# One operation over two PSUM banks in the feed-forward, and the first four tiles of a mixer side by side

## The chip, the core and the metric

The kernel runs on one core of a Trainium2 chip. The metric is the device time of one execution in microseconds, as a median of several. TensorE (PE in the profile) multiplies into PSUM, eight banks of 128 partitions by 512 fp32 columns. VectorE (DVE) and ScalarE (ACT) read PSUM; GpSimd (POOL) works on SBUF alone; SyncE (SP) issues most transfers.

## The reference

A trunk of two layers over T = 528 tokens (16 learned ones and 512 given) of 1024 features:

```
h = layer_norm(ALPHA * h + 0.5 * swiglu(h, ffn1_w_up, ffn1_w_down))
h = layer_norm(ALPHA * h + hybrid_mixer(h, ...))
h = layer_norm(ALPHA * h + 0.5 * swiglu(h, ffn2_w_up, ffn2_w_down))

swiglu(x, w_up, w_down):  gate, up = split(x @ w_up);  (silu(gate) * up) @ w_down
hybrid_mixer:  gated sum of a short convolution and latent attention, both from x @ w_in
```

The feed-forward is 2816 features wide. All is fp32. The 16 learned tokens are dropped from the output.

## The kernel before

Features lie on the partitions: x is held as eight tiles of 128 features by 528 tokens, split into a high part `xh` and a low part `xl` (both fp32r), and `r` is the fp32 residual. Every product is made by `mm3` (lines 91 to 93): three matmuls, high by high, high by low and low by high, into the same PSUM bank. Tokens go in two parts, 256 and 272 wide (or two of 256 in the last mixer and the last feed-forward).

Weights come by SP into `raw` tiles of 128x1024 and `operand` splits them: ACT casts to `wh` (line 111), DVE subtracts to `wl` (line 114). There are four `raw` and four `wh`/`wl` buffers.

A feed-forward (`ffn`) begins with `up_start`, which makes four feature tiles plainly while the norm before it still ends its second token part (`pending`, a generator whose steps are called between the products), and makes the differences of x that the rest needs (`combos`, on POOL, line 338). Then `up_seven` is called nine times, 36 times in the whole kernel. It makes two feature tiles of gate and up for two token halves out of seven half-deep products in place of eight. In order: g1 by x1a into `pa`, g1' by t2 into `pb`, the down projection of earlier features (`mid[0]`, into the other PSUM name `pf`), g2 by x2a on top of `pa`, u1 by t3 on top of `pb`, u2 by nt4 on top of `pb`, s1 by t1 into `pc`, more down projection, g2' by x2b on top of `pc`. Each of these is two groups (j = 0, 1), one to a bank. Between the products DVE and ACT read the sums: after t3 the two adds of line 447 make `u3s` from `pb`, and only then may nt4 add to the same banks:

```
product(pb, operand(u1), t3, False)
for j in range(2):
    V.tensor_tensor(u3s[j], pb[j], m1[j], op=ALU.add)
product(pb, operand(u2), nt4, False)
```

The last down projection adds to `r` (line 572), feeds the sums of the norm (`Norm.add`: squares on ACT at line 262, sums on DVE and POOL at lines 270 and 271), and for its second token part calls a step of the norm of the first part after each tile.

`Norm.run` makes, per token part, the sums over features by matmuls (`token_sums`, line 206), the mean and a reciprocal root by a chain of small DVE operations (lines 282 to 285 and 222 to 231), and lays them out along the tokens by `spread`: ACT scales an identity by one column (line 215) and PE multiplies it by ones (line 216). POOL subtracts the mean (line 293), DVE, ACT and DVE scale and split (lines 301 to 307).

A mixer (`attention`) starts with `first(0)`: four products of x's first token part (`ukv`, `ukr`, two of `ucq`), one after the other, each over all eight tiles of x, with the steps of the norm of the second token part between and after them. Then come two convolution products, the small norms of the latents (`second`, `third`) and `first(1)`.

PSUM is one pool per stage with two names: `ps` (four banks in a feed-forward, six in a mixer) and `pf` (the rest). The tile framework orders each engine's queue by planning the program ahead: among the operations that are ready in its plan it takes the one that comes first in the program. The code holds an operation back where that is not wanted (`tc.issue_after`: behind a given instruction on the same engine). On the chip each queue then runs in that fixed order and waits on semaphores.

Of the kernel before, what the change touches and what calls it, by code (L numbers as in the profile page):

```python
# [18 lines left out]
P = 128  # L19
D = 1024  # L20
# [24 lines left out]
FFN_SCR, MIX_SCR = (4, 14), (6, 8)  # L45
# [6 lines left out]
def trunk(ctx: ExitStack, tc: tile.TileContext, x, meta, f1_up, f1_dn, w_in, b_gate, conv_w, qn_g, w_uq,  # L52
# [12 lines left out]
    @contextmanager  # L65
    def scratch(n, t):

        with tc.tile_pool(name="psp", bufs=1, space=bass.MemoryType.PSUM, reuse_waits="tile") as pool, \
                tc.tile_pool(name="tmp", bufs=t, reuse_waits="tile") as tp:
            banks.append((pool, n))  # L70
            tps.append(tp)
            yield
            banks.pop()
            tps.pop()

    def psum():
        pool, n = banks[-1]
        return pool.tile([P, 512], F32, name="ps", bufs=n)

    def psum2():  # L80
        pool, n = banks[-1]
        return pool.tile([P, 512], F32, name="pf", bufs=8 - n)
# [136 lines left out]
    def rsqrt(v, n, nt, by=float(D)):  # L219
# [10 lines left out]
        V.tensor_scalar(u, u, by / 0.375, 1.875 * by, op0=ALU.mult, op1=ALU.add)  # L230
        return y, V.tensor_tensor(y, u, y, op=ALU.mult)  # L231

    class Norm:
# [10 lines left out]
        def shift_of(self, q0, w):  # L244
# [5 lines left out]
            def shift(i):  # L250
                ps = psum()[:, :w]
# [21 lines left out]
        def run(self, q0, w):  # L273
# [7 lines left out]
            mu, mud, v = small(n, nt), small(n, nt), small(n, nt)  # L281
            V.tensor_copy(mu, mean)
            V.tensor_scalar(mud, mean, float(D), None, op0=ALU.mult)
# [4 lines left out]
            mean, ps = tmp(w), spread(mud, n, nt, psum2())  # L288
# [30 lines left out]

    def project_steps(ps, u, nk, rhs, q0, w, n=4):  # L320
# [8 lines left out]
    def combos(hv, th, tl):  # L329
# [4 lines left out]
        for k in range(KH):  # L334
            a1, b1, a2, b2 = [r[:, m, q:q + w] for m in (k, KH + k) for q in (qa, qb)]
            t1, t2, t3, nt4 = [tmp(w) for _ in range(4)]
            for i, (t, x1, x2) in enumerate(((t1, b1, a1), (t2, b2, t1), (t3, b2, b1), (nt4, a2, t2))):
                G.tensor_tensor(t, x1, x2, op=ALU.subtract)
                split(th[i][:, k, :w], tl[i][:, k, :w], t)

    def up_start(hp, dp, w_up, hv, pending, th, tl, after, begin):
# [12 lines left out]
        def product(o, j, q0, w):  # L354
            ps = psum()[:, :w]
            for k in range(KD):
                mm3(ps, [t[:, k % KH, j * P:(j + 1) * P] for t in o[k // KH]], [t[:, k, q0:q0 + w] for t in (xh, xl)],
                    k == 0, k == KD - 1)
            return ps

        hs = [[hp.tile([P, T], F32R, name=n) for n in ("hh", "hl")] for _ in range(4)]

        def silu(o, j, m, q0, w):
            ps = product(o, j, q0, w)
            sg[m, q0] = tmp(w)
            S.activation(sg[m, q0], ps, AF.Silu)

        def times(o, j, m, q0, w):
            ps = product(o, j, q0, w)
            hh, hl = [t[:, q0:q0 + w] for t in hs[m]]  # L370
# [10 lines left out]
        for part, (q0, w) in enumerate(hv):  # L381
            for f, o in ((silu, g0), (times, u0)):
                for j in range(2):
                    f(o, j, j, q0, w)
                    step(part)
            for j in range(2):
                silu(g1, j, 2 + j, q0, w)
                if after:
                    step(part)
                    step(part)  # L390
# [5 lines left out]
        for q0, w in hv:  # L396
            for j in range(2):
                times(u1, j, 2 + j, q0, w)
                for _ in range(2):
                    next(begin, None)  # L400
        for _ in begin:
            pass
        return hs

    def up_seven(hp, fp, w_up, f, hv, mid, th, tl):
# [9 lines left out]
        def product(ps, u, xs, first):  # L415
            for j in range(2):
                for k in range(KH):
                    mm3(ps[j], [t[:, k, j * P:(j + 1) * P] for t in u], [t[:, k, :] for t in xs],
                        first and k == 0, k == KH - 1, not first)

        def pair():
            return [psum()[:, :w] for _ in range(2)]

        hs = [[hp.tile([P, T], F32R, name=n) for n in ("hh", "hl")] for _ in range(2)]
        m1, u2s, u3s, sg = [[tmp(w) for _ in range(2)] for _ in range(4)]

        pa, pb = pair(), pair()
        product(pa, operand(g1), x1a, True)
        for j in range(2):
            S.copy(m1[j], pa[j])  # L430
# [5 lines left out]
        for j in range(2):  # L436
            V.tensor_tensor(u2s[j], pb[j], m1[j], op=ALU.add)
# [5 lines left out]
        for j in range(2):  # L443
            S.activation(sg[j], pa[j], AF.Silu)
        product(pb, operand(u1), t3, False)
        for j in range(2):
            V.tensor_tensor(u3s[j], pb[j], m1[j], op=ALU.add)  # L447
        product(pb, operand(u2), nt4, False)
        for j in range(2):
            hh, hl = hs[j]  # L450
            V.tensor_tensor(m1[j], pb[j], m1[j], op=ALU.add)
            V.tensor_tensor(sg[j], sg[j], m1[j], op=ALU.mult)
            split(hh[:, qa:qa + w], hl[:, qa:qa + w], sg[j])
        if mid[2]:
            mid[2](hs)
        pc = pair()
# [3 lines left out]
        for j in range(2):  # L460
            V.tensor_tensor(u3s[j], pc[j], u3s[j], op=ALU.add)
# [5 lines left out]
        for j in range(2):  # L467
            hh, hl = hs[j]
            V.tensor_tensor(u2s[j], pc[j], u2s[j], op=ALU.add)
            S.activation(u2s[j], u2s[j], AF.Silu)  # L470
            V.tensor_tensor(u2s[j], u2s[j], u3s[j], op=ALU.mult)
            split(hh[:, qb:qb + w], hl[:, qb:qb + w], u2s[j])
# [736 lines left out]
```

## Time and profile before

| | |
|---|---|
| median of 3 runs | 2213.01 us (2210.86 to 2214.43) |
| the profiled execution | 2215.05 us, of it the span of the profile 2213.0 us |
| mean granted TensorE clock | 0.998 |
| busy in the span | PE 99%, DVE 75%, ACT 44%, POOL 17% |
| DMA | 202.80 MB, mean 92 GB/s |

PE is busy 9 tenths or more in every slice of the page but the first and the last. A matmul's record ends when its pipeline has drained, so records overlap: the rate of matmuls is read from the distance of their starts. "Idle before" counts from the end of the record before.

### The profile page before, as it was taken

How to read it: one execution, taken by the hardware profiler on the slowest of the kernel's cores; microseconds unless marked ns; L12 is line 12 of the kernel's file. 1: busy time of each engine (PE TensorE's matmuls, PEld its weight loads, DVE VectorE, ACT ScalarE, POOL GpSimd, SP SyncE). 2: the span in 40 equal slices, each digit the busy share in tenths (PEclk: the TensorE clock that was granted, in tenths of full speed). 3: DMA queues.
4: the chain of work that ended last, by engine and by line, in shares of the span. 5: the costliest groups of instructions: out<-in, count | busy, mean ns of one | idle time of the engine just before them, and what ended most of it. 6: DMA issues, size and time to landing. Idle time of an engine off the chain costs nothing. (4 is left out here: it accounts for less than half of the span.)

```text
span 2213.0 us, 43882 instructions
## 1 busy us (share of the span) xinstructions
PE 2185.1 (99%) x17989; PEld 2166.9 (98%) x17989; DVE 1663.6 (75%) x3117; ACT 984.7 (44%) x1923; POOL 369.6 (17%) x487
## 2 busy tenths in 40 slices
PE   8999999999999999999999999999999999999998
PEld 8999999999999999999999999999999999999998
DVE  6887788776646788778778877887665568877887
ACT  4343344565533543434453433445655335533341
POOL 3210003301014522000242100033110155100000
PEclk9999999999999999999999999999999999999999
DMA  5333232222233223323323322322222332323322
GB/s 174 96 106 91 91 115 85 77 56 68 68 95 105 68 87 106 105 77 115 105 67 96 105 92 91 115 83 79 56 68 77 94 98 87 95 87 115 96 87 86
DMA packets 240489, 202.80 MB, mean 92 GB/s; under 512 B 6990, under 2 KB 237456, under 8 KB 240288
## 3 DMA queue, kind: packets, MB, share of 16 engines
q1 hardware_dynamic: 237952, 195.65, 29.6%
q0 software_dynamic: 2336, 4.34, 0.8%
q8 instruction: 141, 2.31, 0.4%
q14 instruction: 60, 0.49, 0.1%
HBM read 195.74 MB, written 2.10 MB: 89 GB/s over the span
## 5 line engine op out<-in xcount | busy, mean ns | idle before, releaser
L114 DVE TENSOR_TENSOR wl<-raw,wh 128x1024 fp32r<-128x1024 f32 (+1 forms) x490 | 563.7, 1152 | 235.9 <-ACT wh L111 233.8
L111 ACT CAST wh<-raw 128x1024 fp32r<-128x1024 f32 (+1 forms) x454 | 465.9, 1034 | 575.2 <-PE ps L92 169.4
L91 PE MATMUL ps<-xh,wh 128*128 128x256 f32 (+2 forms) x1760 | 502.2, 285 | 5.2 <-DVE r L572 5.0
L92 PE MATMUL ps<-xl,wh 128*128 128x256 f32 (+2 forms) x1760 | 500.4, 284 | 3.4 <-DVE xl L88 2.8
L93 PE MATMUL ps<-xh,wl 128*128 128x256 f32 (+2 forms) x1760 | 500.3, 284 | 0.0
L91 PEld LDWEIGHTS ps<-xh,wh 128*128 128x128 f32 x1760 | 332.8, 189 | 6.2 <-issue 3.6
L92 PEld LDWEIGHTS ps<-xl,wh 128*128 128x128 f32 x1760 | 332.2, 189 | 5.1 <-DVE xl L88 4.1
L93 PEld LDWEIGHTS ps<-xh,wl 128*128 128x128 f32 x1760 | 332.7, 189 | 0.0
L91 PE MATMUL ps<-th,wh 128*128 128x264 f32 (+1 forms) x1152 | 327.0, 284 | 1.2 <-DVE t L447 1.2
L92 PE MATMUL ps<-tl,wh 128*128 128x264 f32 (+1 forms) x1152 | 325.9, 283 | 0.0
L93 PE MATMUL ps<-th,wl 128*128 128x264 f32 (+1 forms) x1152 | 325.4, 282 | 0.0
L91 PE MATMUL pf<-hh,wh 128*128 128x256 f32 (+1 forms) x864 | 247.3, 286 | 0.0
L93 PE MATMUL pf<-hh,wl 128*128 128x256 f32 (+1 forms) x864 | 246.3, 285 | 0.0
L92 PE MATMUL pf<-hl,wh 128*128 128x256 f32 (+1 forms) x864 | 245.3, 284 | 0.0
L91 PEld LDWEIGHTS ps<-th,wh 128*128 128x128 f32 x1152 | 216.7, 188 | 1.8 <-DVE t L447 1.6
L92 PEld LDWEIGHTS ps<-tl,wh 128*128 128x128 f32 x1152 | 216.9, 188 | 0.0
L93 PEld LDWEIGHTS ps<-th,wl 128*128 128x128 f32 x1152 | 216.5, 188 | 0.0
L91 PE MATMUL pf<-xh,wh 128*128 128x256 f32 (+1 forms) x640 | 187.0, 292 | 0.0
L92 PE MATMUL pf<-xl,wh 128*128 128x256 f32 (+1 forms) x640 | 183.0, 286 | 0.0
L93 PE MATMUL pf<-xh,wl 128*128 128x256 f32 (+1 forms) x640 | 182.3, 285 | 0.0
L91 PEld LDWEIGHTS pf<-hh,wh 128*128 128x128 f32 x864 | 162.8, 188 | 0.0
L93 PEld LDWEIGHTS pf<-hh,wl 128*128 128x128 f32 x864 | 162.8, 188 | 0.0
(323 smaller groups left out, 4836.1 us busy)
## 6 DMA issues: line engine op xcount, KB each, us to landing
raw<-in_ffn_w_up_dram SPq DMA_DIRECT2D x176, 512.0 KB, 3.7
raw<-in_ffn_w_down_dram SPq DMA_DIRECT2D x80, 512.0 KB, 3.4
raw<-in_mix_w_in_dram SPq DMA_DIRECT2D x64, 512.0 KB, 3.8
raw<-in_w_o_dram SPq DMA_DIRECT2D x16, 512.0 KB, 4.0
raw<-in_ffn_w_down_dram SPq DMA_DIRECT2D x16, 256.0 KB, 2.6
raw<-in_w_br_conv_dram SPq DMA_DIRECT2D x8, 512.0 KB, 3.4
raw<-in_w_br_mla_dram SPq DMA_DIRECT2D x8, 512.0 KB, 3.4
out_dram<-r SPq DMA_DIRECT2D x8, 256.0 KB, 2.5
```

The source lines that it names most:

```text
L91: PE.matmul(ps, lhsT=lhs[0], rhs=rhs[0], start=first, stop=False, skip_group_check=more)
L92: PE.matmul(ps, lhsT=lhs[0], rhs=rhs[1], start=False, stop=False, skip_group_check=more)
L93: return PE.matmul(ps, lhsT=lhs[1], rhs=rhs[0], start=False, stop=last, skip_group_check=more)
L111: S.copy(u[0], raw)
L114: V.tensor_tensor(u[1][:, k:k + n], raw[:, k:k + n], u[0][:, k:k + n].bitcast(F32), op=ALU.subtract)
```

## The change

1. In the feed-forward, `ps` is two tiles of two banks (`psum_pair`) in place of four of one. In `up_start`, `up_seven`, `combos` and the last down projection of features, an operation on ACT, DVE or POOL that was done once for each of two feature tiles is done once for both. The temporaries for it are five pairs and four singles in place of 14 singles.
2. The two PSUM names are pools of their own, `pf` in the lower banks in a feed-forward and `ps` in the lower banks in a mixer. The shift of the sums (`shift_of`) and every other sum of the last tokens' down projection use `pf`.
3. `first(0)` of a mixer makes its four products side by side, feature tile by feature tile (`project_all`), and calls the norm's steps after all of them.
4. `spread` multiplies the column itself, repeated along the free side as the stationary operand, by the identity: ACT has no part in it. The mean is laid out by one matmul of ones with the feature sums, and the scaling by D is gone.
5. In the last call of `up_seven` two of the four down projections, not one, leave their second token part for after it.

```
-            dg = tmp(n)[0:n]
-            S.activation(dg, idf[0:n, 0:n], AF.Copy, scale=c[:, i:i + 1])
-            PE.matmul(ps[:, i * n:(i + 1) * n], lhsT=ones[0:n, :], rhs=dg, start=True, stop=True)
+            PE.matmul(ps[:, i * n:(i + 1) * n], lhsT=c[:, i:i + 1].to_broadcast([n, P]), rhs=idf[0:n, 0:n],
+                      start=True, stop=True)
...
-            mean, ps = tmp(w), spread(mud, n, nt, psum2())
+            mean, ps = tmp(w), psum2()[:, :w]
+            PE.matmul(ps, lhsT=ones, rhs=s, start=True, stop=True)
...
+    def project_all(us, nk, rhs, q0, w):
+
+        pss = [psum()[:, :w] for _ in us]
+        for k in range(nk):
+            for ps, u in zip(pss, us):
+                mm3(ps, (u[0][:, k, :], u[1][:, k, :]), (rhs[0][:, k, q0:q0 + w], rhs[1][:, k, q0:q0 + w]),
+                    k == 0, k == nk - 1)
+        return pss
...
-        for k in range(KH):
-            a1, b1, a2, b2 = [r[:, m, q:q + w] for m in (k, KH + k) for q in (qa, qb)]
-            t1, t2, t3, nt4 = [tmp(w) for _ in range(4)]
+        for k in range(0, KH, 2):
+            a1, b1, a2, b2 = [r[:, m:m + 2, q:q + w] for m in (k, KH + k) for q in (qa, qb)]
+            t1, t2, t3, nt4 = [tmp_pair(w) for _ in range(4)]
...
         product(pb, operand(u1), t3, False)
-        for j in range(2):
-            V.tensor_tensor(u3s[j], pb[j], m1[j], op=ALU.add)
+        V.tensor_tensor(u3s, pb, m1, op=ALU.add)
         product(pb, operand(u2), nt4, False)
...
-                    mid = [steps(ci - 1, prev, mp, (0,) if p == 10 and mp == (3,) else (0, 1)) for mp in mps]
+                    mid = [steps(ci - 1, prev, mp, (0,) if p == 10 else (0, 1)) for mp in mps]
...
+                elif j == 1:
+                    rm = r[:, m - 1:m + 1, q0:q0 + w]
+                    V.tensor_tensor(rm, rm, pair, op=ALU.add)
+                    for m1 in (m - 1, m):
+                        norm.add(m1, q0, w)
+                        if part:
+                            step()
...
+                if part == 0:
+                    pss = project_all([ukv, ukr, *ucq], KD, (xh, xl), q0, w)
```

## Rows read from the trace of the kernel before

**Rows 1.** The page's part 1: busy us, share of the span, instructions.

```profile
PE 2185.1 (99%) x17989; PEld 2166.9 (98%) x17989; DVE 1663.6 (75%) x3117; ACT 984.7 (44%) x1923; POOL 369.6 (17%) x487
```

**Rows 2.** Waits of PE: who waited for whom, us in total, times, longest us.

```profile
PE ps L91 <- DVE r L572: 5.0, 3, 1.8
...
PE ps L92 <- DVE xl L88: 2.8, 6, 0.8
...
PE pf L216 <- ACT t L215: 1.3, 2, 0.6
PE ps L91 <- DVE t L447: 1.2, 2, 0.7
...
PE ps L92 <- DVE xl L307: 0.5, 2, 0.3
```

**Rows 3.** Windows, one call of `up_seven`: busy us by engine, clock, DMA.

```profile
139.58:171.71 32.13, 32.13 (x266) 32.13 (x265) 25.54 (x42) 12.46 (x19) 0.00 (x0) 1.00 0.32 99
```

**Rows 4.** Timeline of PE, t3 to nt4: start us, us, what, idle before.

```profile
177.41 0.28 PE L93 MATMUL ps<-th,wl 128*128 128x264 f32 x1
177.52 0.28 PE L91 MATMUL ps<-th,wh 128*128 128x264 f32 x1
```

**Rows 5.** Timeline of DVE, the second add of line 447 there.

```profile
177.72 0.43 DVE L447 TENSOR_TENSOR t<-ps,t 128x264 f32<-128x264 f32 x1 [0.25 <-PE ps L93]
```

**Rows 6.** Groups of DVE by shape: busy us, mean ns, idle before.

```profile
L88 DVE TENSOR_TENSOR hl<-t,hh 128x264 fp32r<-128x264 f32 x108 | 49.1, 454 | 0.6
...
L88 DVE TENSOR_TENSOR tl<-t,th 128x264 fp32r<-128x264 f32 x48 | 26.9, 634 | 0.1
...
L447 DVE TENSOR_TENSOR t<-ps,t 128x264 f32<-128x264 f32 x54 | 23.1, 428 | 5.3 <-PE ps L93 5.1
...
L983 DVE CUSTOM_DVE_ANT_0 ps<-ps,strip 128x512 f32<-128x512 f32 x8 | 5.9, 734 | 0.0
```

**Rows 7.** Timeline of all engines, t3 to nt4 of a first call of `up_seven`.

```profile
79.97 0.28 PE L93 MATMUL ps<-th,wl 128*128 128x264 f32 x1
...
80.28 0.43 DVE L447 TENSOR_TENSOR t<-ps,t 128x264 f32<-128x264 f32 x1
...
80.76 0.39 PE L91 MATMUL ps<-th,wh 128*128 128x264 f32 x1 [0.52 <-DVE t L447]
```

**Rows 8.** Timeline of all engines, a mean laid out in `up_start`.

```profile
754.58 2.04 ACT L215 ACTIVATE t<-idf,sm 68x68 f32<-68x68 f32 x8
...
755.39 0.33 PE L216 MATMUL pf<-t,ones 68*128 68x68 f32 x2
755.53 0.37 PE L93 MATMUL ps<-xh,wl 128*128 128x256 f32 x1
...
756.57 0.36 PE L93 MATMUL ps<-xh,wl 128*128 128x256 f32 x1
```

**Rows 9.** Timeline of PE where the first mixer starts.

```profile
378.39 0.29 PE L93 MATMUL ps<-hh,tl 128*128 128x272 f32 x1
...
380.27 0.35 PE L91 MATMUL ps<-xh,wh 128*128 128x256 f32 x1 [1.59 <-DVE r L572]
...
383.39 0.39 PE L92 MATMUL ps<-xl,wh 128*128 128x256 f32 x1 [0.27 <-DVE xl L307]
```

**Rows 10.** Timeline of DVE at the first mixer's start.

```profile
379.70 0.42 DVE L572 TENSOR_TENSOR r<-r,ps 128x272 f32<-128x272 f32 x1
...
382.86 0.48 DVE L307 SCALAR_TENSOR_TENSOR xl<-r,prm,xh 128x256 fp32r<-128x256 f32 x1
```

**Rows 11.** Timeline of DVE, the chain of the norm's second part in that mixer.

```profile
385.11 0.16 DVE L282 COPY sm<-pf 68x4 f32<-68x4 f32 x1 [1.42 <-PE pf L206]
...
386.27 1.33 DVE L223 TENSOR_SCALAR sm<-sm 68x4 int32<-68x4 int32 x1
...
389.19 0.16 DVE L231 TENSOR_TENSOR sm<-sm 68x4 f32<-68x4 f32 x1
```

**Rows 12.** Windows, after the wait between the two feed-forwards.

```profile
1116.70:1120.10 3.40, 3.40 (x18) 3.40 (x17) 1.27 (x4) 0.43 (x1) 1.56 (x2) 0.50 0.95 297
```

More of the change, by code (lines that the diff above doesn't have):

```diff
@@ L66, in scratch @@
     def scratch(n, t):
-        with tc.tile_pool(name="psp", bufs=1, space=bass.MemoryType.PSUM, reuse_waits="tile") as pool, \
-                tc.tile_pool(name="tmp", bufs=t, reuse_waits="tile") as tp:
-            banks.append((pool, n))
+        with ExitStack() as own:
+            two = {}
+            for name, b in (("ps", n), ("pf", 8 - n))[::1 if n > 4 else -1]:
+                p = own.enter_context(tc.tile_pool(name=name + "p", bufs=1, space=bass.MemoryType.PSUM,
+                                                   reuse_waits="tile"))
+                if name == "ps" and t == FFN_SCR[1]:
+                    two["pp"] = lambda p=p: p.tile([P, 2, 512], F32, name="pp", bufs=2)
+                else:
+                    two[name] = lambda p=p, b=b, name=name: p.tile([P, 512], F32, name=name, bufs=b)
+            tp = own.enter_context(tc.tile_pool(name="tmp", bufs=t, reuse_waits="tile"))
+            banks.append(two)
             tps.append(tp)
@@ L280, in run @@
             ex2 = token_sums(ps, 2 * nt, (q,), n, nt)
[L281 removed]
+            mu, v = small(n, nt), small(n, nt)
             V.tensor_copy(mu, mean)
[L283 removed]
             V.tensor_tensor(v, mu, mu, op=ALU.mult)
@@ L352, in half, with product, silu, times @@
             return us
[L354 to L358, printed above, removed]
-            return ps
[L361 to L365, printed above, removed]
+        def product(o, q0, w, each):
+            ps = psum_pair(w)
+            for j in range(2):
+                for k in range(KD):
+                    mm3(ps[:, j], [t[:, k % KH, j * P:(j + 1) * P] for t in o[k // KH]],
+                        [t[:, k, q0:q0 + w] for t in (xh, xl)], k == 0, k == KD - 1)
+                each()
+            return ps
+        hs = [hidden(hp) for _ in range(2)]
+        def silu(o, m, q0, w, each):
+            ps = product(o, q0, w, each)
+            sg[m, q0] = tmp_pair(w)
             S.activation(sg[m, q0], ps, AF.Silu)
-        def times(o, j, m, q0, w):
-            ps = product(o, j, q0, w)
-            hh, hl = [t[:, q0:q0 + w] for t in hs[m]]
+        def times(o, m, q0, w, each):
+            ps = product(o, q0, w, each)
+            hh, hl = [t[:, :, q0:q0 + w] for t in hs[m]]
             t = sg.pop((m, q0))
@@ L382, in up_start @@
             for f, o in ((silu, g0), (times, u0)):
-                for j in range(2):
[L384 to L390, printed above, removed]
+                f(o, 0, q0, w, lambda: step(part))
+            silu(g1, 1, q0, w, lambda: after and (step(part), step(part)))
             if part == 0:
@@ L396, in up_start @@
         for q0, w in hv:
[L397 to L400, printed above, removed]
+            times(u1, 1, q0, w, lambda: (next(begin, None), next(begin, None)))
         for _ in begin:
             pass
-        return hs
+        return tiles_of(*hs)
     def up_seven(hp, fp, w_up, f, hv, mid, th, tl):
@@ L417, in product @@
                 for k in range(KH):
-                    mm3(ps[j], [t[:, k, j * P:(j + 1) * P] for t in u], [t[:, k, :] for t in xs],
+                    mm3(ps[:, j], [t[:, k, j * P:(j + 1) * P] for t in u], [t[:, k, :] for t in xs],
                         first and k == 0, k == KH - 1, not first)
[L421 to L427, printed above, removed]
+        hh, hl = hidden(hp)
+        hs = tiles_of((hh, hl))
+        m1, u2s, u3s, sg = [tmp_pair(w) for _ in range(4)]
+        pa, pb = psum_pair(w), psum_pair(w)
         product(pa, operand(g1), x1a, True)
-        for j in range(2):
-            S.copy(m1[j], pa[j])
+        S.copy(m1, pa)
         s1 = raw_tile(fp).rearrange("p (k c) -> p k c", c=256)
@@ L435, in up_seven @@
         product(pb, operand(g1), t2, True)
-        for j in range(2):
-            V.tensor_tensor(u2s[j], pb[j], m1[j], op=ALU.add)
+        V.tensor_tensor(u2s, pb, m1, op=ALU.add)
         mid[0]()
@@ L459, in up_seven @@
             mid[3]()
-        for j in range(2):
-            V.tensor_tensor(u3s[j], pc[j], u3s[j], op=ALU.add)
+        V.tensor_tensor(u3s, pc, u3s, op=ALU.add)
         if not mid[2]:
@@ L466, in up_seven @@
             mid[3]()
[L467 to L472, printed above, removed]
+        V.tensor_tensor(u2s, pc, u2s, op=ALU.add)
+        S.activation(u2s, u2s, AF.Silu)
+        V.tensor_tensor(u2s, u2s, u3s, op=ALU.mult)
+        split(hh[:, :, qb:qb + w], hl[:, :, qb:qb + w], u2s)
         return hs
@@ L809, in first, with products @@
                 n, nt = TOKENS[w]
-                ps = psum()[:, :w]
-                project(ps, ukv, KD, (xh, xl), q0, w)
+                if part == 0:
+                    pss = project_all([ukv, ukr, *ucq], KD, (xh, xl), q0, w)
+                else:
+                    pss = (psum()[:, :w] for _ in range(4))
+                def products(u):
+                    ps = next(pss)
+                    if part:
+                        project(ps, u, KD, (xh, xl), q0, w)
+                    return ps
+                pss = iter(pss)
+                ps = products(ukv)
                 S.copy(ckv[:, q0:q0 + w], ps)
```

60 lines of the change are left out of this document (29 added, 31 removed).

## The prediction
> **What bounds the kernel now.** I read the page's busy shares first: PE 99%, DVE 75% [rows 1]. Then one call of `up_seven` by windows: PE is busy 32.13 of 32.13 us and starts a matmul every 32.13/266 = 0.121 us, while DVE has 25.54 us of work and ACT 12.46 [rows 3]. So in these 36 calls, 36 x 32.13 = 1157 us and over half the span, nothing but the number of matmuls sets the time, and work saved on DVE or ACT is worth nothing there. What is left to win lies in PE's waits, and the list of them is short: 5.0 us for line 572, 2.8 and 0.5 us for the low parts of x, 1.3 us for ACT's scaled identities, 1.2 us for line 447 [rows 2]. The reader is to see that these are single places at the seams of the stages, not something that repeats; and that a change here can lose far more by one new wait in each of the 36 calls of `up_seven` than it can win.
>
> **The change part by part**, against the profiled execution's 2215.05 us (a span of 2213.0 and 2.05 around it).
>
> *Merged operations: what they save.* A call of `up_seven` has 18 DVE operations of 128x264, which become 9 of 2x264. One takes 428 ns; the nearest row for the merged one, PSUM in, 512 columns, takes 734 [rows 6], so a pair saves about 0.12 us, a call 9 x 0.12 = 1.1 us and the kernel 36 x 1.1 = 40 us of DVE. Its worth is nought: PE has no gap in that call [rows 3].
>
> *Merged operations: what they cost.* Almost all have cover: `pa` has t2 and the down projection (48 to 72 matmuls, at 0.121 us at least 5.8 us) before it is added to; `pc` has a down projection; a new call's first product (24 matmuls, 2.9 us) covers the read of the pair that its second product takes over. The hidden tiles come later by some 0.3 us for each of five merged operations, 1.5 us, under down projections of 24 matmuls and more; in the last call, where the last down projection needs them at once, the second projection that is now left for later adds 24 matmuls of 2.9 us.
>
> One place has no cover in the program: t3, the add of line 447, nt4 into the same two banks. Before, the first bank is added up while PE fills the second: nt4 starts 0.11 us after t3's last matmul [rows 4], while the second add begins only 0.20 us after nt4's start [rows 5], and nobody waits for it until nt4's second half. Now nt4's first matmul waits for the one add over both banks: it can start no sooner than the second add did, 177.72, takes 0.73 [rows 6], and PE follows 0.05 later (in the first call of all, the add that ended at 80.28 + 0.43 let PE start at 80.76 [rows 7]). 177.72 + 0.73 + 0.05 - 177.52 = 0.98 us, 36 times: 35 us if PE stands still. On DVE the sums of line 451 are queued behind, with slack.
>
> But the planner puts ready work in such holes. Where the mean's four pieces waited for ACT, PE's queue reads two records of line 216, one matmul of the next product, two records, and so on [rows 8]: single matmuls were drawn in. Here the next product in the program, t1 into `pc`, is ready: its weights are split some 10 us ahead, as all are with four buffers, and the banks of `pa` have been read by then. 0.98 us is 8 of its 24 matmuls. What is left is the error of the plan. In rows 8 it erred to the safe side: ACT's eight scaled identities took 2.04 us from 754.58, so the first was there by about 754.9, and PE came to it at 755.39. In rows 7 it erred by 0.67 us (79.97 + 0.12 to 80.76), with DVE behind. Between 0 and 0.98 us a call I take 0.03, near the row with a filled hole: **+1.1 us**, bounds 0 and 35.
>
> The Trainium skill has a rule against this change (Perfetto Trace Analysis, section Optimizing Scalar/DVE Operations): larger operations help where the engine is saturated, and where it is not but makes bubbles on another, operations are to be broken up. DVE at 75% is not saturated [rows 1], so by the rule the merge buys nothing and the 35 us are the price; that is rival 1. The trace agrees with its first half; whether the bubble stays is the planner's doing.
>
> *The start of a mixer.* The last matmul of the feed-forward starts at 378.39, the first of the mixer at 380.27; the next would have been due at 378.52, so 1.75 us are lost, and 0.27 more at 383.39 for the last low part of x [rows 9]. The first wait ends with the read of a PSUM bank at 379.70 + 0.42 [rows 10]; in the new layout the mixer's first four banks are the feed-forward's `pf` banks, idle by then. Side by side, a feature tile of x feeds 12 matmuls, 1.45 us; the last tile, written at 382.86 + 0.48 = 383.34 [rows 10], is needed 84 matmuls after 378.52, at 388.7. Both waits go, and the second mixer has them too (line 572's three waits are 5.0 us, the longest 1.8, and 1.59 is this one: 1.6 is left [rows 2, 9]; line 307's are two of 0.27): 2 x 2.0 = **-4.0 us**, bounds -4.2 and 0.
>
> *What is late next there.* The norm's steps now come behind all 96 matmuls (11.6 us). Before, its chain of small operations, 389.35 - 385.11 = 4.24 us, of it 1.33 in one slow instruction [rows 11], ran under three products of 24 matmuls, 8.7 us. After, only the convolutions' 48 matmuls (5.8 us) and the laying out of the mean can cover it, and only if their weights are split in time, on the engine that runs the chain. Between nothing and 2.5 us a mixer I take 1.0: **+2.0 us**, bounds 0 and 5.
>
> *Spreads.* ACT's 1.3 us of waits [rows 2] go; the reciprocal root itself is due next, and it is what ACT waited for: **-1.3**, bounds -2.5 (waits too short to show) and 0. The mean over 272 tokens took 756.57 - 755.39 less three matmuls, 0.82 us, in eight records [rows 8]; one matmul over as many columns costs the same at most and saves perhaps 0.3, in four such runs: **-1.2**, bounds -2 and 0. The scaling by D, one small DVE operation of 0.16 us in the chain, is in the rounding.
>
> *Between the two feed-forwards* the longest of line 572's waits, 1.8 us [rows 2], is followed by 3.40 us at a clock of 0.50 [rows 12]: 1.7 us more. The pair's bank comes free earlier, but the first product there needs x's last tile as before: of 3.5 us I take back **-2.0**, bounds -3.5 and 0.
>
> *The second token part in `up_start`.* The 2.8 us for low parts of x [rows 2] should shrink with a shorter norm. Against it, POOL's operations of `combos` are now twice as long, and DVE's splits beside them already take 634 ns where the like take 454 [rows 6]. I take **-0.5**, bounds -2.8 and +6 (three such places, 2 us each).
>
> Sum: 1.1 - 4.0 + 2.0 - 1.3 - 1.2 - 2.0 - 0.5 = -5.9 us; 2215.05 becomes 2209.2. The profiled execution lies 2.0 us above the median of 2213.01, so I predict a median of 2207.
>
> **The rivals.**
>
> 1. *PE stands at t3 and nt4* (slower). For: no cover in the program; 0.67 us was lost there where DVE came late [rows 7]. Against: the filled holes [rows 8]. With the other terms at -7.0, it decides from 7.0/36 = 0.19 us a call, and slower by 0.2% is reached at 0.32. With 0.5 us a call the time is 2213 - 7 + 18 = 2224; with all 0.98, 2241.
> 2. *The seams only move* (no change). The exposed chain after the side-by-side products takes back 2 x 2.0 of the mixers' gain and the longer POOL operations 2 to 4 us in `up_start`: 2213 - 5.9 + 2 + 3 = 2212. For: a chain of 4.24 us against cover that hangs on DVE [rows 11], and the slow splits [rows 6]. Against: it was shorter by 1.2 us but for one instruction, and holes get filled.
> 3. *All seams close* (faster). No loss at nt4 or after the products, and every bound of gain reached: -4.2 - 2.5 - 2 - 3.5 - 2.8 = -15, 2198. For: each wait is named in rows 2. Against: x's last tile comes from DVE, which is full in those stretches.
>
> **How the numbers follow.** Forecast 0.46 (own range 2202 to 2212), rival 1 0.18, rival 2 0.22, rival 3 0.14. The range: 2196 takes in rival 3, 2225 rival 1 up to half its price. 0.2% is 4.4 us, about what a measurement here can tell from no change: faster means below 2208.6. Of the forecast three quarters lie there (0.34), with rival 3 0.48. Same: 0.10 of the forecast and 0.20 of rival 2, 0.30. Slower: rival 1, and 0.02 each of the forecast and of rival 2, 0.22.
>
> **What would show it.** Nt4: the queue of PE after t3's last matmul; some 8 matmuls of t1 before nt4's first, and a list of waits in which line 447's successor stays below 2 us, show the forecast right; the same place with an idle of 0.3 us or more, 36 times, shows rival 1. Mixers: the first matmul within 0.2 us of the feed-forward's last, then 96 in a row; an idle of over 1 us between the token sums and the convolutions shows the chain exposed. `up_start`: waits for the low parts of x above 2.8 us in sum show the long POOL operations. Between the feed-forwards: a clock of 1.00 throughout. A window over one call of `up_seven` longer than 32.5 us in which PE is not idle would make all of this wrong.

## Result: slower, 1.016 of the time before

The changed kernel takes 2248.97 us (median of 4 runs, 2246.43 to 2250.0) against 2213.57 for the kernel before beside it: a ratio of 1.0161, 95% interval 1.0149 to 1.0174. The forecast was 2207, with a range of 2196 to 2225. The span grew from 2213.0 to 2247.7 us. Part 1 of the page after (busy us, share of the span, instructions) stands against [rows 1]:

```profile
PE 2199.1 (98%) x17953; PEld 2176.7 (97%) x17953; DVE 1635.5 (73%) x2695; ACT 940.8 (42%) x1599; POOL 375.4 (17%) x455
```

DVE and ACT have less to do, by 28 us (40 were forecast for DVE) and 44 us, and it is worth nothing, as forecast. PE's waits after, against [rows 2] (who waited for whom, us in total, times, longest):

```profile
PE pp L104 <- DVE tt L402: 6.4, 4, 2.0
PE pp L104 <- ACT hh L101: 5.2, 4, 1.6
PE pf L227 <- DVE sm L243: 3.5, 2, 1.8
...
PE pp L105 <- DVE xl L101: 2.5, 3, 0.9
PE pp L104 <- DVE tt L462: 2.2, 4, 0.6
PE pp L104 <- ACT wh L124: 2.1, 2, 1.1
PE ps L104 <- DVE r L587: 2.1, 2, 1.1
PE pp L105 <- DVE hl L101: 1.7, 3, 0.7
```

Counts of two to four are places that occur once in a stage. Nothing occurs 36 times. (Line 402 is `times` in `up_start`, 101 the split, 243 the end of the reciprocal root, 462 and 464 the sums of t3 and nt4, 587 the last sums.) Behind most groups of waits, not behind all, PE ran for a while at the lower of its two clocks. Leaving out the first and last microseconds of the span, the trace before has one such stretch, 3.40 us [rows 12]; windows of the trace after (busy us by engine, clock, DMA share, GB/s) show seven:

```profile
65.50:68.90 3.40, 3.40 (x18) 3.40 (x17) 3.15 (x4) 2.43 (x3) 0.00 (x0) 0.51 0.11 39
352.30:355.70 3.40, 3.40 (x18) 3.40 (x17) 1.11 (x2) 0.72 (x2) 0.01 (x1) 0.50 0.02 5
406.90:410.30 3.40, 3.40 (x18) 3.40 (x17) 3.30 (x6) 0.32 (x1) 3.40 (x4) 0.50 0.44 98
...
1471.80:1478.60 6.80, 5.99 (x26) 5.70 (x27) 2.66 (x5) 0.84 (x3) 0.00 (x0) 0.50 0.29 77
1526.50:1533.30 6.80, 5.75 (x27) 5.78 (x28) 6.54 (x15) 0.82 (x3) 5.39 (x5) 0.50 0.23 59
sum 30.60, PE 28.68 PEld 28.43 DVE 19.95 ACT 7.29 POOL 8.80; mean PE 4.10 PEld 4.06 DVE 2.85 ACT 1.04 POOL 1.26
```

In 30.60 us at half speed at most 15.3 are lost, against 1.7 before: up to 13.6 of the 35 us are the clock's, paid on top of waits of 0.5 to 2 us, where PE stood before the clock fell. The rest is PE standing.

Stages, read from the starts of PE's matmuls (us). "First call" is the first product with a t; "last call" runs from its product with t2. The runs e5 to e15 are described below.

| stretch | before | after | e5 | e10 | e18 | e15 |
|---|---|---|---|---|---|---|
| start to the first call of feed-forward 1 | 65.46 | 69.35 | 69.15 | 65.56 | 65.17 | 69.32 |
| eight calls of feed-forward 1 | 257.94 | 257.98 | 257.96 | 257.92 | 257.89 | 257.96 |
| its last call to the mixer's first product with ckn | 104.18 | 112.60 | 108.26 | 106.49 | 104.27 | 104.97 |
| last call of feed-forward 2 to the first call of 3 | 113.12 | 118.70 | 118.04 | 120.06 | 111.89 | 113.61 |
| as the third row, feed-forward 3 and its mixer | 104.29 | 113.21 | 107.68 | 106.46 | 103.77 | 104.88 |
| last call of feed-forward 4 to PE's end | 51.09 | 54.02 | 52.16 | 51.75 | 51.57 | 52.89 |

The steady calls take what they took. The loss is at the ends: 3.9 us in `up_start`, 8.4 and 8.9 from the last call into the two mixers, 5.6 between feed-forwards 2 and 3, 2.9 at the end, together 29.7; some 5 more are spread over heads, merges and the last feed-forward. It lies where I had counted on cover or on a gain. What the stretches at the lower clock cost is in these figures, up to 1.7 us for each 3.40.

### The profile page after: what moved, and what is told of

Read it like the earlier page. It is cut to its first block, busy times and chain, and to the rows that moved or that the text cites. A ratio compares the mean times of both kernels' runs of the same rounds, so it can differ in the third digit from the quotient of the medians.

```text
span 2247.7 us, 43001 instructions
## 1 busy us (share of the span) xinstructions
PE 2199.1 (98%) x17953; PEld 2176.7 (97%) x17953; DVE 1635.5 (73%) x2695; ACT 940.8 (42%) x1599; POOL 375.4 (17%) x455
## 4 chain that ended last, share of the span: by engine, by line
PE 88%; DVE 7%; POOL 1%; ACT 1%; DMA 1%; issue 1%; SPq 0%; DVEq 0%; ACTq 0%; POOLq 0%
PE pp L104 13%; PE pp L105 13%; PE pp L106 13%; PE pf L104 10%; PE pf L106 9%; PE pf L105 9%; PE ps L104 6%; PE ps L105 6%; PE ps L106 6%; DVE wl L127 1%; POOL tt L359 1%; DVE xl L101 1%; DMA raw<-in_ffn_w_down_dram 1%; DVE r L313 1%; ACT wh L124 1%
## 5 line engine op out<-in xcount | busy, mean ns | idle before, releaser
L104 PE MATMUL pp<-xh,wh 128*128 128x264 f32 (+2 forms) x1376 | 393.7, 286 | 8.3 <-DVE tt L402 6.1
L105 PE MATMUL pp<-xl,wh 128*128 128x264 f32 (+2 forms) x1376 | 391.2, 284 | 2.5 <-DVE xl L101 2.5
L106 PE MATMUL pp<-xh,wl 128*128 128x264 f32 (+2 forms) x1376 | 391.8, 285 | 0.2 <-DVE wl L127 0.2
L104 PE MATMUL pp<-th,wh 128*128 128x264 f32 (+1 forms) x1152 | 328.7, 286 | 2.6 <-DVE tt L462 2.2
L105 PE MATMUL pp<-tl,wh 128*128 128x264 f32 (+1 forms) x1152 | 326.7, 284 | 0.0
L106 PE MATMUL pp<-th,wl 128*128 128x264 f32 (+1 forms) x1152 | 319.9, 282 | 0.0
L104 PEld LDWEIGHTS pp<-xh,wh 128*128 128x128 f32 x1376 | 260.4, 189 | 10.1 <-DVE tt L402 6.7
L105 PEld LDWEIGHTS pp<-xl,wh 128*128 128x128 f32 x1376 | 260.1, 189 | 3.4 <-DVE xl L101 3.3
L106 PEld LDWEIGHTS pp<-xh,wl 128*128 128x128 f32 x1376 | 260.5, 189 | 0.4 <-DVE wl L127 0.4
L105 PEld LDWEIGHTS pp<-tl,wh 128*128 128x128 f32 x1152 | 217.1, 188 | 0.0
```

The lines of the kernel that those rows point to most:

```text
L104: PE.matmul(ps, lhsT=lhs[0], rhs=rhs[0], start=first, stop=False, skip_group_check=more)
L105: PE.matmul(ps, lhsT=lhs[0], rhs=rhs[1], start=False, stop=False, skip_group_check=more)
L106: return PE.matmul(ps, lhsT=lhs[1], rhs=rhs[0], start=False, stop=last, skip_group_check=more)
```

## Experiments

Ratios are to the kernel before, run on the same chip; "+" is us above that kernel's median there.

**e1: side by side alone.**

```
+                if part == 0:                                   # on the kernel before
+                    pss = project_all([ukv, ukr, *ucq], KD, (xh, xl), q0, w)
...
-                project(ps, ukv, KD, (xh, xl), q0, w)
```

> The kernel before with one part of the change alone: the first token part's four products of a mixer run side by side (project_all), all else as before. Theory A (the chain of the norm is exposed behind the 96 matmuls, and the clock falls with it): each mixer's stretch from its first matmul to the first product of ckn grows from 47.3 to about 51 us, two waits of 1 us or more behind the products, 2213.5 + 8 = 2221 less the start wait of 2 x 1.9 that goes: 2216 to 2222. Rival B (the products are innocent; the chain is late because the merged operations upstream made it late): the start waits go and nothing comes in their place, 2207 to 2211, the stretch below 47 us.

2229.46 us, ratio 1.008 (1.0064 to 1.0095): +17.3, more than either theory gave. The stretch from the last product with a t to the first with ckn grew from 69.4 to 78.5 us. The waits at the mixer's start stayed, and a second one of 1.5 us came behind each (PE's waits for the last sums, line 581 there, are five of 8.1 us; before, three of 5.0). Behind the 96 matmuls PE stands for the norm:

```profile
399.44 0.69 PE L216 MATMUL pf<-t,ones 68*128 68x68 f32 x2 [2.77 <-ACT t L215]
```

and then runs on at half speed (window: busy us by engine, clock):

```profile
399.40:406.00 6.60, 6.56 (x32) 6.57 (x32) 6.48 (x11) 2.17 (x6) 6.60 (x7) 0.53 0.33 102
```

The trace of e1 has four stretches at a clock of 0.50 (from 381.7, 398.8, 1494.4 and 1511.5), 20.5 us together against 3.4 before: up to 8.5 of the 17.3 us are the clock's. So theory A holds in its mechanism; its price was too small.

**e2: the last call single again**, its last sums too, and one late projection.

```
+        def each(f, *ts, **kw):
+            for t in [[t[:, j] for t in ts] for j in range(2)] if mid[2] else [ts]:
+                f(*t, **kw)
...
-        V.tensor_tensor(u3s, pb, m1, op=ALU.add)
+        each(V.tensor_tensor, u3s, pb, m1, op=ALU.add)
```

> The changed kernel with the last call of up_seven (p = 10 of each feed-forward) one operation per bank again, the same for the last sums, and only the fourth projection's second token part left for later, as before. Theory A (in the last call the merged chain sum, product, split is on the path, as the last down projection needs the hidden tiles at once): the stretch from t2 of that call to the next stage goes back from 61 to 57 us, four times 3 to 4.5 us less, 2249 - 15 = 2231 to 2238, and PE's waits for the hidden tiles' splits (5.2 us) and for the sums of line 462 go. Rival B (it is the two pair slots, not the length of the operations, that hold PE there): under 4 us in all, 2245 to 2249, the waits as before. Rival C (steady calls carry the loss): no more than 1 us.

2249.0 us, 1.0168 (1.0153 to 1.0184): no gain. The last call itself is 1 us shorter, and what it won comes back behind it, 3.4 us of wait before feed-forward 3 alone. Theory A of that run fell; the time fits its rivals B and C alike.

**e3: `combos` and `up_start` single again.**

```
-                G.tensor_tensor(t, x1, x2, op=ALU.subtract)
-                split(th[i][:, k:k + 2, :w], tl[i][:, k:k + 2, :w], t)
+                for j in range(2):
+                    G.tensor_tensor(t[:, j], x1[:, j], x2[:, j], op=ALU.subtract)
+                    split(th[i][:, k + j, :w], tl[i][:, k + j, :w], t[:, j])
```

> The changed kernel with the operations of combos and up_start on one feature tile each again (same pair buffers and banks; every operation half as long, twice as many). Theory A (long DVE splits next to long POOL operations make the first call's pair slot late): the three waits of 2.18 us at the end of up_start go, and the half clock behind two of them: 4 to 10 us less, 2239 to 2245; the splits take about half of 1.6 to 2.3 us. Rival B (only five pair buffers hold POOL and DVE back, whatever the length of an operation): the waits stay within 0.5 us of 2.18 and the time within 2 us of 2249.

2247.56 us, 1.0164 (1.0149 to 1.018). The waits of 2.18 us became 1.45 and a new one of 0.7 came behind each. (These are from start to start of two matmuls, less one matmul; as idle time the lists have 2.02 for the first.) The time is rival B's, the waits are neither's. The length of the operations is not it.

**e4: the spread alone, on the kernel before** (the first two pieces of the diff shown above).

> The kernel before with one part of the change alone: the spread without ACT's scaled identities, and the mean laid out by one matmul over the sums. Theory A (these were the terms -1.3 and -1.2 of the forecast): 2209.5 to 2212.5, no wait of line 216 for ACT, and the laying out of the mean near 0.5 instead of 0.8 us. Rival B (the part of the norm that is late is the reciprocal root, and PE waits as long for that): within 1 us of 2213.5. Rival C (the broadcast weights are slow for PE): slower, 2215 or more.

2212.37 us, 1.0006 (0.9996 to 1.0015): nothing. The wait for ACT is gone and two others have grown:

```profile
PE ps L92 <- DVE xl L88: 5.7, 6, 1.7
...
PE ps L206 <- POOL u L718: 1.3, 2, 0.7
```

**e5: the changed kernel, mixer as before.**

```
-                if part == 0:
-                    pss = project_all([ukv, ukr, *ucq], KD, (xh, xl), q0, w)
-                else:
-                    pss = (psum()[:, :w] for _ in range(4))
+                pss = (psum()[:, :w] for _ in range(4))
```

> The changed kernel with the mixer's first four products one after the other again. The side-by-side products alone cost the kernel before 17 us (2212.2 to 2229.5), 9 us in each of the two stretches from the feed-forward's last quarter products to the first product of ckn (69.4 to 78.4 us). In the changed kernel that stretch is 74.7 us. Theory A (they are about a third of the loss here too): the stretch returns to about 69.5 us twice, 2249 - 10 = 2237 to 2241, and the 1.91 us wait for the reciprocal root goes. Rival B (in the changed kernel the norm comes late for another reason, the last feed-forward call): the stretch stays above 73 us and the time above 2245.

2236.62 us, 1.0115 (1.0098 to 1.0132), +25.9: theory A, 0.4 us below its range. The stretch is 70.4 and 70.1 us, and the wait for the reciprocal root (1.77 us of idle time, line 243) is gone. 9.5 of the 35.4 us are the side-by-side products'. The stretches at the lower clock fell from 30.6 to 13.7 us in the two traces, so up to 8.5 of the 9.5 are paid through the clock.

**e6: every operation single, pairs of banks and buffers kept** (e2's `each` for all calls, e3's edit, single last sums).

> The changed kernel with every merged operation of the feed-forward one per feature tile again, but the pairs of banks and of buffers kept: a pair is still handed on whole. Theory A (long operations make the waits): the feed-forwards' share of the loss, some 18 us, goes, and what stays is the side-by-side products: 2228 to 2233. Rival B (the pairs make them: two slots of two banks where four single banks were, five pairs and four single buffers where fourteen single ones were; no operation's length matters): 2244 to 2250, the last call's stretch from t2 to its last quarter product 36.5 us or more against 34.8 before.

2243.42 us, 1.0151 (1.0136 to 1.0166), +32.7: rival B, 0.6 us below its range. The merged operations, which the change is named after, cost 2.7 us, less than the two intervals leave open.

**e7: e6 with e5's edit and one late projection.**

> As the run with all operations single, and in addition the mixer's products one after the other and one projection left for later in the last call, both as before. What is left of the change is the pairs of banks and buffers, and the spread. Theory A (long operations): 2211 to 2216, no difference from before. Rival B (pairs): 2228 to 2238, the three to five us that each feed-forward lost still lost.

2234.41 us, 1.0105 (1.009 to 1.012), +23.7: rival B. With no operation merged, the pairs alone carry two thirds of the loss.

**e9: e2 with two late projections.**

> As the run with the last call's operations single, which won nothing, but with two projections left for later, as in the changed kernel. There the last call's stretch was 36.8 us against 37.8 (before: 34.8), and what it won was lost again behind it, with waits of 0.5 to 3.6 us for hidden tiles and banks. Theory A (the missing fill of the second late projection took the gain back): 2240 to 2245. Rival B (the gain is not there: PE's order follows the two slots of pairs): 2247 to 2251, the same waits of 1 us and more.

2243.62 us, 1.015 (1.0135 to 1.0166), +32.9 against e2's +36.8: theory A in sign, but the intervals overlap. The last call, from its t2 to its last product with a t, takes 34.5 us here (after 37.8, before 34.8), and the loss sits behind it.

**e10, e11, e12: which pairs.** A pair becomes two single tiles, for the buffers (e10), the banks (e11), or both (e12), all from e7. (The hidden tiles `hh` and `hl`, which the change also makes in pairs, stay pairs in all three.)

```
+    class Two:
+        def __init__(self, make):
+            self.of = [make() for _ in range(2)]
+        def __getitem__(self, at):
+            return self.of[at[1]]
...
-        return tps[-1].tile([P, 2, 272], F32, name="tt", bufs=FFN_PAIRS)[:, :, :w]
+        return Two(lambda: tmp(w))
...
-        return banks[-1]["pp"]()[:, :, :w]
+        return Two(lambda: psum()[:, :w])
```

> As e7_pairs_alone (2234.4, with 2210.7 before), but the working buffers are fourteen single ones again; only the PSUM banks are still handed on in pairs (two slots of two). Theory A (the two slots of PSUM make the feed-forwards' waits): 2230 to 2236, the waits at the end of up_start and in the last call as in e7. Theory B (the five buffer pairs hold POOL and DVE back in combos, and DVE is late for all that follows): 2211 to 2217, the 2.2 us waits gone. Between the two by shares: the first feed-forward's start (69.35 us to its first t2, 65.46 before) belongs to B, the last calls (37 us against 34.8) to A.

> As e7_pairs_alone, but the PSUM banks are eight single ones again, four for the products and four for the rest; the working buffers stay five pairs and four singles. Theory A (PSUM's slots): 2211 to 2217. Theory B (the buffer pairs): 2228 to 2236.

> Banks and buffers both single: what stays of the change is the order in which the program lists the work (both products of a pair before the operations on either), the spread, and the feed-forward's four other banks placed first, so that a mixer's first banks are idle ones. Theory (pairs carry it all): 2205 to 2211, and the two waits of 1.76 us at the start of a mixer shrink to the wait for x. Rival (the order of listing makes ACT and DVE serve a tile later): 2216 to 2234, and e10 and e11 both stay above 2220.

e10 2229.47 us, 1.0081 (1.0066 to 1.0096), +17.7. e11 2213.3, 1.0008 (0.9998 to 1.0017). e12 2213.21, 1.0008 (0.9999 to 1.0018), +1.4. So e10 is theory A's and e11 too; e12 lies between the two ranges given for it: without the pairs the loss is gone, but nothing of the forecast's gain has come. The pairs of banks cost 16.3 us. The buffer pairs cost nothing by themselves, and 6.0 where the banks are paired too (e7 less e10, whose intervals just overlap). The same sum in e10 and in e12 shows what a pair does. DVE in e10, where the product's first bank is full with the matmul of 158.06 and its second with that of 159.52 (start us, us, instruction, idle before):

```profile
157.88 1.23 DVE L135 TENSOR_TENSOR wl<-raw,wh 128x1024 fp32r<-128x1024 f32 x1 [0.27 <-ACT wh L132]
159.84 0.43 DVE L469 TENSOR_TENSOR t<-pp,t 128x264 f32<-128x264 f32 x1 [0.73 <-PE pp L114]
```

PE there:

```profile
158.06 0.28 PE L114 MATMUL pp<-xh,wl 128*128 128x264 f32 x1
...
159.52 0.28 PE L114 MATMUL pp<-xh,wl 128*128 128x264 f32 x1
```

The operation is on the first bank alone, DVE is idle for 0.73 us, and still it starts only when the second bank's last matmul (159.52 + 0.28) has ended. In e12 the first sum runs before the product's last matmul, which starts at 158.21:

```profile
157.71 0.42 DVE L466 TENSOR_TENSOR t<-ps,t 128x264 f32<-128x264 f32 x1
158.53 0.43 DVE L466 TENSOR_TENSOR t<-ps,t 128x264 f32<-128x264 f32 x1 [0.40 <-PE ps L111]
```

Here a pair was one object to its reader. Whether the framework or the chip sets this, the traces don't show.

**e13: the norm's steps inside the side-by-side products**, on e12.

```
+            if k in (1, 3):          # in project_all's loop over feature tiles
+                each()               # the norm's next step
```

> As e12_singles, with the mixer's first four products side by side as in the change, but the norm's first two steps listed after the second and the fourth of the eight feature tiles, in the midst of the 96 matmuls, where they stood before. Theory A (side by side is slow because the norm's chain comes behind all 96 matmuls): the stretch from the last quarter product to the first of ckn is 67 to 69 us instead of 78.4 (before 69.4), and the time equals e12's or is up to 4 us below. Rival B (side by side is slow because all four results come at the same time and the copies, the rotary and the squares stand in one queue): the stretch stays above 73 us, 8 to 16 us above e12.

2213.66 us, 1.001 (1.0001 to 1.002), +1.9 against e12's +1.4: theory A in the time, and the chain runs under products again (below); the stretch up to ckn is 69.3 and 70.9 us (67 to 69 expected, 78.5 in e1). Its gain at the mixer's start did not come: the first product still waits 2.30 us at 378.85.

**e18: the last sums in single banks**, on e10.

```
-                ps = pair[:, j] if final else psum2()[:, :w]
+                ps = psum2()[:, :w]
+                if final:
+                    pair = (*pair, ps) if j else (ps,)
```

> As e10_psum_pairs (2229.5; with single banks, e12, 2213.2), but the last down projection's sums take single banks from the other four; up_start and up_seven keep pairs. Theory A (a pair costs where two products become one chain of 24 matmuls and the ready half of the second cannot be drawn ahead, that is in the last sums): most of the 16 us goes, 2213 to 2219; the last call from t2 on takes 34.8 instead of 36.8 us and the third feed-forward's first product no longer waits 3.55 us. Rival B (it costs in the products of the calls, whose first bank is now read only when both are written): 2225 to 2230.

2215.91 us, 1.0019 (1.0009 to 1.0028), +3.3: theory A. 14.4 of the 16.3 us are the last down projection's pairs. Up to 3.4 of them went through the clock: 10.2 us at 0.50 in e10's trace, 3.4 in e18's. PE's waits in e10:

```profile
PE pp L113 <- DVE hl L109: 4.2, 9, 1.6
...
PE pp L112 <- DVE r L611: 3.4, 1, 3.4
...
PE pp L112 <- DVE t L465: 2.6, 3, 0.9
```

and in e18:

```profile
PE pf L113 <- DVE hl L109: 3.4, 6, 1.6
...
PE ps L112 <- DVE r L611: 1.4, 1, 1.4
```

PE's queue in the last call says why (matmuls in a row; A to D are last sums, the first six of each use older hidden tiles and are ready, the rest need the ones just made):

```
e10: t3 24, A 6, nt4 24, B 6, A 1, B 1, A 17, B 17, C 24, D 24, t1 24
e18: t3 24, a 6, b 3, nt4 24, b 3, c 6, d 6, t1 1, a 1, b 1, c 1, d 1, t1 2, a 5, b 5 ...
```

In e10 A to D are pairs, in e18 single tiles. A pair's 24 matmuls stay one chain: its second tile's six ready matmuls are behind the first tile's unready ones. Between nt4 and the first matmul that needs a new hidden tile there are 6 ready ones (0.73 us) in e10 and 16 (1.9 us) in e18. And even these 6 come late in e10:

```profile
345.15 0.77 DVE L465 TENSOR_TENSOR t<-pp,t 128x264 f32<-128x264 f32 x2 [0.54 <-PE pp L114]
345.97 0.39 PE L112 MATMUL pp<-hh,th 128*128 128x256 f32 x1 [0.86 <-DVE t L465]
```

There are two slots for pairs. B takes the banks of t3 and nt4, so its first matmul waits 0.86 us until the sums of nt4 (line 465) have read them; the list has three such waits, 2.6 us. In e18 the last sums take the other four banks. That mends the chain, the slot and the reader's wait at once, so how the 14.4 us divide among the three is not shown.

**e15: the changed kernel with both repairs** (e13's and e18's), merged calls kept.

> The changed kernel with all its merged operations in the calls, but the norm's first two steps listed inside the side-by-side products, as in e13, and the last sums in single banks, one sum for each. Theory (these two places carry the loss, the merged operations of the calls nothing): 2249 - 12.6 - 12 to 16 = 2220 to 2225. Rival (merged operations of combos and up_start still hold the first call, 2.2 us three times with the clock behind it, and the last call's merged hidden tiles): 2228 to 2236.

2227.04 us, 1.0071 (1.0056 to 1.0087), +14.5: between the two ranges given; 21 of 35 us are back. Mixers and the seam between the feed-forwards are within 0.8 us of before (table); the start is not, and the wait for `times` stays as after:

```profile
PE pp L104 <- DVE tt L404: 6.8, 5, 2.0
```

**e16: three slots**, 2 + 2 + 2 banks for pairs and 2 single, in the changed kernel.

```
-                    two["pp"] = lambda p=p: p.tile([P, 2, 512], F32, name="pp", bufs=2)
+                    two["pp"] = lambda p=p: p.tile([P, 2, 512], F32, name="pp", bufs=3)
```

> The changed kernel with three pairs of banks for the products and two single banks for the rest, instead of two and four. Theory A (the whole-pair wait is the matter, not the number of slots): the time stays within 5 us of 2249, some waits at the end of up_start go and others come where the down projections have two banks only. Rival B (two slots are too few): 2232 to 2240, the 2.18 us waits and those of the last call gone.

2274.03 us, 1.0281 (1.0266 to 1.0296), outside both ranges. The other projections, down to two banks, now wait; eight calls take 268.1 us. It doesn't say whether a third slot would help by itself.

**e19: e15 with `combos`, `up_start` and the last call single.**

> As e15_after_two_repairs (2227.0), but the operations of combos, of up_start and of the last call of up_seven are one per feature tile again; merged are now only those of the other calls of up_seven (eight in each feed-forward, seven in the last). Theory A (the rest is at the ends): 2214 to 2219, as e18 (2215.9), which has pairs of banks and no merged operation; the 2.18 us waits shrink to 1.45 and the eight calls take 258 us as before. Rival B (the rest is in the steady calls): above 2223.

2224.25 us, 1.0057 (1.0041 to 1.0074), +12.9: a miss by 5 us for A. The steady calls (258.06, 258.03, 258.04 us) are innocent, so B isn't the reason either. Two us are at the first call; the rest is in pieces of 1 to 3 us, the largest, 3.2, between the first product with ckn and the first call of feed-forward 2. The clock hides part of what was won: this trace has three stretches of 3.4 us at 0.50, e15's and the one before have one, so up to 3.4 of the 12.9 us are the clock's.

## Why the prediction was wrong, step by step

From after to e5, e7, e10 and e12 the kernels undo the change one part at a time: 35.4, 25.9, 23.7, 17.7, 1.4 us above before. Side by side 9.5, merged operations with the second late projection 2.2, buffer pairs beside bank pairs 6.0, bank pairs 16.3, what is left 1.4. The split depends on the order: on the kernel before, side by side alone costs 17.3. Only 9.5 and 16.3 are clear of the intervals. The clock's share differs: the traces have 30.6, 13.7, 6.8, 10.2 and 10.2 us at 0.50, so the bank pairs' 16.3 owes nothing to it.

1. *t3 to nt4, +1.1: right.* The planner filled the hole, with eight matmuls of t1 as forecast. Timeline after, against [rows 4, 5]; the fill runs from 148.64, the sum ends at 149.55, nt4 starts at 149.61:

```profile
148.64 0.29 PE L104 MATMUL pp<-th,wh 128*128 128x264 f32 x1
148.84 0.71 DVE L462 TENSOR_TENSOR tt<-pp,tt 128x528 f32<-128x528 f32 x1 [0.59 <-PE pp L106]
...
149.61 0.38 PE L104 MATMUL pp<-th,wh 128*128 128x264 f32 x1
```

A call is as long as in [rows 3]:

```profile
145.74:177.90 32.16, 32.16 (x266) 32.12 (x265) 24.26 (x31) 12.18 (x14) 0.00 (x0) 1.00 0.32 99
```

Rival 1, the one I gave for slower, did not happen there. In the last call of each feed-forward nt4 does wait, 0.6 us four times (line 462 in the list, 2.2 us). That the whole loss, 35 us, is what rival 1 would have cost is chance.

2. *"Almost all have cover", and "24 matmuls of 2.9 us" in the last call: the step that failed.* I priced a longer operation, at nothing. The price was in the pair, 16.3 us for the banks: its reader waits for both of them, its products are one chain in PE's queue, and there are only two slots. In steady calls other projections fill this (eight calls of feed-forward 1 take 257.98 us, before 257.94). In the last call 6 ready matmuls stood where I had counted 24, and the trace after shows DVE's chain of nt4's sum, product and split, with PE standing for both parts of the split:

```profile
346.57 0.70 DVE L464 TENSOR_TENSOR tt<-pp,tt 128x528 f32<-128x528 f32 x1
...
348.48 0.70 DVE L465 TENSOR_TENSOR tt<-tt 128x528 f32<-128x528 f32 x1
...
349.21 0.63 ACT L101 CAST hh<-tt 128x528 fp32r<-128x528 f32 x1 [0.82 <-DVE tt L465]
349.90 0.38 PE L104 MATMUL pp<-hh,wh 128*128 128x256 f32 x1 [1.53 <-ACT hh L101]
350.30 0.70 DVE L101 TENSOR_TENSOR hl<-tt,hh 128x528 fp32r<-128x528 f32 x1
351.06 0.38 PE L105 MATMUL pp<-hl,wh 128*128 128x256 f32 x1 [0.66 <-DVE hl L101]
```

Between 347.27 and 348.48 DVE splits a weight (1.23 us). This chain looks like the cause; that the length of its operations alone is not is what e2 and e6 showed. The rule that I cited from the Trainium skill (Perfetto Trace Analysis, section Optimizing Scalar/DVE Operations), that breaking operations up may help where an engine isn't saturated but makes bubbles, points the way the result went, but not to its means. Here breaking them up (e6) returned 2.7 us, within the intervals.

3. *Start of a mixer, -4.0, and the exposed chain, +2.0: failed.* Together they came to about +9.5 us with e5, +17.3 with e1. I saw that the steps come "behind all 96 matmuls" and took 1 us a mixer between 0 and 2.5. After, DVE waits 10.82 us for the token sums, and PE for the chain, against [rows 11]:

```profile
400.13 0.37 ACT L838 COPY ckv<-ps 128x256 f32<-128x256 f32 x1 [9.42 <-PE ps L106]
...
401.44 1.99 ACT L124 CAST wh<-raw 128x1024 fp32r<-128x1024 f32 x2
402.10 0.16 DVE L294 COPY sm<-pf 68x4 f32<-68x4 f32 x1 [10.82 <-PE pf L219]
...
404.44 0.16 DVE L243 TENSOR_TENSOR sm<-sm 68x4 f32<-68x4 f32 x1
...
404.74 1.08 PE L227 MATMUL pf<-idf,sm 68*128 68x68 f32 x8 [1.77 <-DVE sm L243]
...
411.00 0.39 PE L104 MATMUL pf<-xh,wh 128*128 128x256 f32 x1 [0.46 <-ACT cs L728]
```

The cover I counted, the convolutions, needs weights that ACT casts only at 401.44: the casts are queued behind the products' copies, for which ACT stood idle 9.42 us. So 1.77 us stand uncovered, the clock falls, and a wait for line 728's copy follows. In e13 the same chain begins at 384.41 and ends at 387.58, under the products, and no wait for it is in PE's list:

```profile
384.41 0.16 DVE L299 COPY sm<-pf 68x4 f32<-68x4 f32 x1 [2.96 <-PE pf L224]
...
387.42 0.16 DVE L248 TENSOR_TENSOR sm<-sm 68x4 f32<-68x4 f32 x1
```

The gain was not there either. The first matmul comes at once, as forecast, but the second product waits 1.11 us for the last sums (line 587), which the list after has in place of line 572's; in e13 the wait is at the first. Why a bank that should be idle waits I did not settle.

4. *Between the feed-forwards, -2.0: failed*, +5.6 from the last call on. The low clock there is gone, as hoped (the window at 1116.70 has no successor between 1099.8 and 1188.5), but both its neighbours are new. With single last sums (e18) the stretch is 111.9 us, 1.2 under before. But e1, which changes nothing at this seam, has 111.6: its wait there, 1.83 us at 1123.16, drew no stretch at the lower clock, while the 1.79 us before did. So the 1.7 us that I priced for the clock came and went between traces with the same seam.

5. *Spreads, -1.3 and -1.2: failed.* ACT's wait went and nothing was won (e4): the low parts of x took its place.

6. *`up_start`, -0.5, bounds -2.8 and +6: the bound, not the value.* +3.9 in the first feed-forward. The wait I named, for low parts of x, is 2.5 and did not matter; late is the pair that `times` reads, behind splits that DVE runs at 1186 ns beside POOL (groups by shape), and the clock behind it. The group, then the timeline:

```profile
L101 DVE TENSOR_TENSOR tl<-tt,th 128x528 fp32r<-128x528 f32 x24 | 27.7, 1186 | 2.7 <-ACT th L101 1.5
```

```profile
64.08 0.67 DVE L402 TENSOR_TENSOR tt<-tt,pp 128x512 f32<-128x512 f32 x1
...
64.81 0.39 PE L104 MATMUL pp<-xh,wh 128*128 128x264 f32 x1 [2.02 <-DVE tt L402]
```

All with single operations, the first call is at 67.67 with pairs of buffers and of banks (e7), at 65.56 with pairs of banks (e10) and at 64.39 with pairs of buffers (e11). So some 2.1 of the 3.9 us are the five buffer pairs', and only with banks in pairs; the other 1.7 are about what the stretch at 0.50 from 65.50 costs, which e7 does not have.

What stays open: e15 and e19 keep 13 to 15 us that the parts of the ladder do not name one by one. In e15 the waits for `times`, 6.8 us, are the largest piece; its clock fell no longer than before. And no kernel tried beats the one before: the best are within 0.1% of it.

## What to carry to other kernels

Two tiles made into one saved instructions here, but a reader of one half waited for the other, and PE's queue had fewer ready products to choose from. Price that at the ends of a stage, where little else is ready, not in the steady loop. When products are put side by side, list the long chain that hides under them at its old place; and count a wait's price with the clock that falls behind it.

## What was not expected of the hardware

A short wait at the end of a stage was often followed by 3.4 or 6.8 us at a granted clock of 0.50 (the lower level): the 2.18 us at 64.81 by 3.40 us, so that it cost 1.7 more. The same wait at 811.09 was not followed by any (the window 811 to 815 shows 1.00). PE's share misleads here: 98% busy after, and 28.7 us of it in seven stretches at half speed.
